# A scheduler's rule for a port shared by two engines, and an order searched anew: two transformer blocks on one core

## The chip, the cores and the metric

The kernel runs on one core of one Trainium2 chip. The metric is device time in microseconds (us), the median of three runs of the kernel before. A profiled execution gives the trace. Five engines matter: TensorE (PE; its weight loads are listed as PEld), VectorE (DVE), ScalarE (ACT), GpSimd (POOL) and SyncE (SP), which here only issues DMAs.

## The reference, cut to what matters

Batch 1, 256 tokens, width 1024, all float32. A first block with two layers (a sparse attention, then a block-wise attention) and a second block (feed-forward, two attentions side by side, feed-forward):

```python
cond = silu(c)
for i in range(2):                                   # first block
    shift, scale, gate = split(cond @ ada_w[i] + ada_b[i], 3)      # ada_w[i]: 1024 x 3072
    h = rms_norm(x, norm_g[i]) * (1 + scale) + shift               # "modulation"
    y = nsa_mixer(h, ...) if i == 0 else moba_mixer(h, ...)
    x = x + gate * y
# second block
x = x + 0.5 * swiglu(rms_norm(x, ffn1_norm), ...)    # 1024 -> 2816 -> 1024
h = rms_norm(x, mix_norm); proj = h @ w_in
x = x + (sigmoid(g_mla) * (mla(...) @ w_branch_mla) + sigmoid(g_fox) * (fox(...) @ w_branch_fox)) @ w_o
x = x + 0.5 * swiglu(rms_norm(x, ffn2_norm), ...)
```

In the attentions a softmax row p is divided by its sum (in the sparse attention also multiplied by a gate) before the product with the values.

## The kernel before

**Arithmetic.** A weight tile is loaded as float32 into `raw` (128x1024, six buffers), split into a high part `hi` (a rounded copy, ACT or DVE) and a low part `lo` = raw - hi (a subtraction, DVE or POOL). Activations lie transposed in `hT`, also as high and low part. A product is three matmuls (`mm3`): high by high, high by low, low by high. 512 columns of one take PE some 0.23 us at the higher clock.

**Stages.** The start: load x, norm statistics of each half of the tokens (`norm_stats`: ACT squares, DVE `nms`, POOL `rstd`), scale (`norm_x`), transpose on PE into `xT`. `mod0(q)` for q = 0..3 then makes a quarter of the first layer's modulation: `ada_mod(0, q)` (line 913) loads four tiles of `ada_w`, each 128x1024, `ada_sum` multiplies them with `sT` (silu of c) on PE, and `modulate` applies the result to two of the eight 128-wide pieces of `hT`. Each quarter is followed by three products with pieces of `nsa_w_in`. Later come the sparse attention (`nsa_scores`, `nsa_values`), its output product, the second layer (`moba_scores`, `moba_values`), feed-forward 1, the two attentions of the second block, feed-forward 2. Before each feed-forward `norm_T` makes h = x * rstd * gain (two DVE operations of 512 columns for each half of the tokens, tiles `t4` from `x` and `sh`), PE transposes it, ACT and DVE write `hT`. Nothing else is left to multiply there: PE has only the end of the product before as cover.

**What sets the order.** The code does not issue instructions itself; it calls a `Recorder`, which notes each operation, its predecessors and a cost. `order()` (line 380) then plays the program through on a model of the engines and takes, step by step, the instruction that can start first; among those ready at one time the one of lowest `rank`. `ORDER` (a permutation of some 1,150 units of work) sets the ranks, and `FLIPS` says for each operation that two engines could do (`either`, line 221) which one does it. Both tables were found by a search over the model's result. `emit` issues in that order, and each engine then runs its own list strictly in order. So everything depends on how the model sees waits: a wait that it does not see is not planned around.

**The port in the model.** `shared_port` (line 308) marks the operations of DVE and POOL that cannot run at the same time: every POOL operation with a tensor input in SBUF, and those of DVE with two such inputs, or plain copies and scalings from SBUF. A marked operation may start when `port[other]` is past. The lines in `order()` are

```python
if ops[i][6]:
    s = max(s, port[other[e]])
...
if c is None or (s, rank[i]) < c[:2]:
    c = (s, rank[i], i, e)
```

When POOL has waited for some time and DVE comes to the port just as it is given free, both have the same start `s`, and the lower rank goes.

**Clock and DMA in the model.** PE runs at 2.4 or 1.2 GHz; line 524 gives it the higher level where the work of the stretch before was at least 3060 (columns). `DMA_BPNS` is what all DMAs move in a nanosecond, 290 bytes.

**Row scalings.** `nsa_scores` (line 1310) and `moba_scores` (line 1485) scale each row block of `P` with its own `scale_rows`: 8 or 4 blocks of 128x128 where only one block of keys is seen (nk = 1, the first half of the tokens), else blocks of 128x256 or 128x128.

Of the kernel before, what the change touches and what calls it, by code (L numbers as in the profile page):

```python
# [11 lines left out]
AF = mybir.ActivationFunctionType  # L12
# [26 lines left out]
def shape_constants():  # L39
# [133 lines left out]
class Recorder:  # L173

    ENG = ("pe", "act", "dve", "pool", "sp")
    DMA_PRE = 1500.0
    DMA_LAT = 700.0
    DMA_BPNS = 290.0  # L180

    SETS = {AF.Exp: 1, AF.Tanh: 1, AF.Sin: 2, AF.Silu: 3}
    SET_LOAD = 1283.0

    def __init__(self, nc):
        self.nc = nc
# [1782 lines left out]
```

## Time and profile before

| | us |
|---|---|
| runs shown | 914.24, 917.89, 919.01 |
| median | 917.89 |
| profiled execution | 916.27 |
| its span (first to last instruction) | 914.4 |
| PE busy in the span | 871.4 |
| DVE, ACT, POOL busy | 662.3, 399.1, 406.0 |

PE is busy for 95% of the span; the mean granted clock is 0.981 of the higher level. "Busy" of DVE and POOL includes the time for which a started operation waits inside for the other of the two. Almost all instructions have the line of the recorder's `emit` (591, or 589 for a tiled group), so they are told apart by their tiles: `tp` is a PSUM bank for transposes and small products, `t` is `t4`, `w` is `w2`, `b` is `b4`, `f` is `f4`.

### The profile page before, as it was taken

To read this page: it belongs to the slowest core of one execution; us is meant where nothing else is said; L and a number is where in the kernel's file an instruction comes from. 1 tells how busy PE (TensorE), PEld (TensorE's weight loads), DVE (VectorE), ACT (ScalarE), POOL (GpSimd) and SP (SyncE) were. 2 spreads that over 40 slices of the span, in tenths; PEclk is the share of its full clock that TensorE was granted. 3 is DMA by queue.
4 is the path that set the end of the run, shared out by engine and by line. 5 is a ranking of instruction groups with operands and counts; after the bars stand their busy time and mean duration, and the time that the engine had idled before them with its cause. 6 is when DMAs were issued, how large, how long until landed. Compare 5 with 4: busy or idle time off the path is not lost.

```text
span 914.4 us, 13923 instructions
## 1 busy us (share of the span) xinstructions
PE 871.4 (95%) x4953; PEld 706.2 (77%) x4953; DVE 662.3 (72%) x1411; ACT 399.1 (44%) x858; POOL 406.0 (44%) x302
## 2 busy tenths in 40 slices
PE   5999999999999989999999999989999899999997
PEld 2579677767787758888888887877778888888886
DVE  5257889898788977766467676787897756666665
ACT  4245567875738742133412454464462323232221
POOL 3356442331354241155563736644535345451552
PEclk9899989999999998999999999999999999999999
DMA  8986656678444672656566556364435455656541
GB/s 256 320 273 185 229 163 179 186 229 265 157 139 128 220 233 90 194 184 202 167 186 199 163 164 176 119 179 144 140 116 190 132 182 179 214 176 195 160 162 47
DMA packets 129732, 165.08 MB, mean 181 GB/s; under 512 B 8055, under 2 KB 93433, under 8 KB 129662
## 3 DMA queue, kind: packets, MB, share of 16 engines
q1 hardware_dynamic: 129224, 164.07, 57.9%
q8 instruction: 39, 0.64, 0.3%
q14 instruction: 31, 0.25, 0.1%
q10 hardware_dynamic: 438, 0.12, 0.1%
HBM read 162.59 MB, written 1.05 MB: 179 GB/s over the span
## 4 chain that ended last, share of the span: by engine, by line
PE 78%; DVE 9%; ACT 4%; DMA 3%; issue 2%; POOL 2%; SPq 0%; POOLq 0%; ACTq 0%; DVEq 0%
PE mm L591 42%; PE tp L591 17%; PE s L591 9%; PE o L591 4%; PE o L589 3%; DVE lo L591 2%; PE s L589 2%; DVE t L591 2%; POOL lo L591 1%; ACT t L591 1%; DVE hi L591 1%; ACT w L591 1%; DVE w L591 1%; PE tp L589 1%; ACT hi L591 1%
## 5 line engine op out<-in xcount | busy, mean ns | idle before, releaser
L591 POOL TENSOR_TENSOR lo<-raw,hi 128x1024 fp32r<-128x1024 f32 (+2 forms) x94 | 232.9, 2483 | 236.2 <-DVE hi L591 121.9
L591 ACT ACTIVATE hi<-raw 128x1024 fp32r<-128x1024 f32 (+2 forms) x148 | 154.0, 1045 | 191.3 <-PE mm L591 77.8
L591 DVE TENSOR_TENSOR lo<-raw,hi 128x1024 fp32r<-128x1024 f32 (+3 forms) x155 | 196.8, 1275 | 29.5 <-ACT hi L591 28.6
L591 PE MATMUL mm<-hi,hT 128*128 128x512 f32 (+4 forms) x736 | 203.6, 354 | 2.6 <-DVE t L591 1.9
L591 PE MATMUL mm<-hT,hi 128*128 128x512 f32 (+1 forms) x576 | 170.1, 356 | 0.4 <-DVE w L591 0.4
L591 PEld LDWEIGHTS mm<-hi,hT 128*128 128x128 f32 x736 | 131.2, 193 | 24.2 <-issue 2.8
L591 PE MATMUL mm<-lo,hT 128*128 128x512 f32 (+4 forms) x368 | 129.4, 353 | 1.3 <-POOL lo L591 0.7
L591 PE MATMUL mm<-hT,lo 128*128 128x256 f32 x448 | 122.5, 288 | 1.0 <-DVE lo L591 1.0
L591 PE MATMUL tp<-hT,hi 128*128 128x512 f32 x320 | 115.8, 397 | 0.0
L591 PEld LDWEIGHTS mm<-hT,hi 128*128 128x128 f32 x576 | 102.5, 195 | 14.6 <-issue 1.6
L591 PE MATMUL mm<-hi,b 128*128 128x512 f32 (+2 forms) x272 | 96.2, 407 | 1.9 <-DVE b L591 1.8
L591 DVE CAST hi<-raw 128x1024 fp32r<-128x1024 f32 (+1 forms) x101 | 81.8, 816 | 21.0 <-PE s L591 6.8
L591 PEld LDWEIGHTS mm<-hT,lo 128*128 128x128 f32 x448 | 85.9, 193 | 6.6 <-DVE lo L591 2.5
L591 PE MATMUL tp<-hT,lo 128*128 128x256 f32 x320 | 83.7, 282 | 0.8 <-POOL lo L591 0.8
L591 PEld LDWEIGHTS mm<-lo,hT 128*128 128x128 f32 x368 | 71.1, 193 | 11.7 <-DVE lo L591 2.8
L591 PE MATMUL s<-hi,b 128*128 128x512 f32 x208 | 71.6, 395 | 0.0
L591 PEld LDWEIGHTS tp<-hT,hi 128*128 128x128 f32 x320 | 59.3, 188 | 11.6 <-ACT hi L591 0.2
L591 PEld LDWEIGHTS tp<-hT,lo 128*128 128x128 f32 x320 | 59.8, 188 | 5.6 <-POOL lo L591 1.3
L591 POOL TENSOR_TENSOR rstd<-hms,nhalf 128x4 f32<-128x4 f32 (+2 forms) x32 | 43.8, 1367 | 43.4 <-DVE hms L591 42.5
L591 PEld LDWEIGHTS mm<-hi,b 128*128 128x128 f32 (+1 forms) x272 | 51.6, 191 | 14.8 <-DVE b L591 2.4
L591 PE MATMUL mm<-lo,b 128*128 128x512 f32 (+1 forms) x136 | 55.3, 407 | 1.1 <-DVE lo L591 1.1
L591 ACT ACTIVATE t<-tt,nb 128x128 f32<-128x128 f32 (+1 forms) x96 | 42.5, 446 | 12.1 <-DVE nb L591 11.9
(281 smaller groups left out, 1389.5 us busy)
## 6 DMA issues: line engine op xcount, KB each, us to landing
raw<-in_ffn_w_gate SPq DMA_DIRECT2D x44, 512.0 KB, 4.6
raw<-in_ffn_w_up SPq DMA_DIRECT2D x44, 512.0 KB, 4.3
raw<-in_ffn_w_down SPq DMA_DIRECT2D x44, 512.0 KB, 4.1
raw<-in_ada_w SPq DMA_DIRECT2D x64, 256.0 KB, 4.6
raw<-in_nsa_w_in SPq DMA_DIRECT2D x26, 512.0 KB, 6.7
raw<-in_moba_w_in SPq DMA_DIRECT2D x20, 512.0 KB, 4.1
raw<-in_w_in SPq DMA_DIRECT2D x18, 512.0 KB, 4.1
raw<-in_ada_w SPq DMA_DIRECT2D x16, 512.0 KB, 4.3
```

The source lines that it names most:

```text
L589: self.engines[eng].matmul(**{n: real(v) for n, v in c.items()})
L591: getattr(self.engines[eng], fn)(*[real(v) for v in a], **{n: real(v) for n, v in k.items()})
```

## The change

Six things change; what is computed does not.

1. In `order()` an instruction that waits for the port keeps the time at which it asked (`asks`), and among engines whose next instructions have equal starts the one that asked first goes, before the rank.
2. The model's constants: the clock's condition goes from 3060 to 1200, `DMA_BPNS` from 290 to 320.
3. The `ada_w` tiles of the first layer go to `f4` (six buffers of the same size, which hold attention tensors later) and not to `raw`.
4. `modulate`'s DVE operation can also be given to ACT.
5. Where nk = 1, the 8 (sparse) or 4 (block-wise) scalings of 128x128 become one product of 128x1024 or 128x512 with the broadcast sums. There are four of each.
6. `ORDER` and `FLIPS` are searched anew on this model.

```diff
 ORDER = [
-    123, 454, 132, 942, 11, 5, 30, 249, 13, 99, 467, 4, 14, 950, 681, 307, 254, 0, 137, 46, 3, 10, 42, 274, 263, 21,
...
+    148, 10, 7, 304, 34, 695, 926, 234, 172, 452, 280, 446, 934, 660, 46, 238, 455, 649, 147, 652, 22, 666, 258, 0,
...
-    DMA_BPNS = 290.0
+    DMA_BPNS = 320.0
+    BUSY = 1200.0
...
-                        if ops[i][6]:
-                            s = max(s, port[other[e]])
                         for nm in of_bank[i]:
                             for e2, t in bank.get(nm, {}).items():
                                 if e2 != e:
                                     s = max(s, t + LAT[e2][e])
-                        if c is None or (s, rank[i]) < c[:2]:
-                            c = (s, rank[i], i, e)
+
+                        asks = s
+                        if ops[i][6]:
+                            s = max(s, port[other[e]])
+                        if c is None or (s, rank[i]) < (c[0], c[2]):
+                            c = (s, asks, rank[i], i, e)
...
-                    f = 2.4 if ticks.get(w - 1, 0.0) >= 3060.0 else 1.2
+                    f = 2.4 if ticks.get(w - 1, 0.0) >= self.BUSY else 1.2
...
         S.activation(hT[:, c, 0, ts], src, AF.Identity, scale=g, bias=sh)
-        V.tensor_scalar(u, src, g, sh, op0=OP.mult, op1=OP.add)
+        rec.either(("dve", "tensor_scalar", (u, src, g, sh), dict(op0=OP.mult, op1=OP.add)),
+                   ("act", "activation", (u, src, AF.Identity), dict(scale=g, bias=sh)))
...
-        ada_mod(0, q)
+        ada_mod(0, q, "f4")
...
-        for r in range(4):
+        if nk == 1:
+
+            V.tensor_tensor(P, P, sums.unsqueeze(3).unsqueeze(4).to_broadcast([128, 4, nb_, 1, 128]), op=OP.mult)
+        for r in range(4 if nk > 1 else 0):
...
-        for r in range(4):
+        if nk == 1:
+            V.tensor_tensor(P, P, sums.unsqueeze(2).unsqueeze(3).to_broadcast([128, 4, 1, 128]), op=OP.mult)
+        for r in range(4 if nk > 1 else 0):
             scale_rows(P[:, r], sums[:, r:r + 1], "act")
```

**The start, PE's list.** x0 and x1 are the two halves of the tokens. Before, PE's list after the first row broadcast (`w2_0` by `ones`) holds the sixteen transposes of x (`cst` by `w2`), then six groups of `ada_w` tiles:

```order
L591 MATMUL tp_1_120<-cst_0_123,w2_1_86 128x128 x4
L591 MATMUL tp_0_119<-cst_0_123,w2_2_87 128x128 x4
L591 MATMUL tp_1_120<-cst_0_123,w2_3_88 128x128 x4
L591 MATMUL tp_0_119<-cst_0_123,w2_4_89 128x128 x4
L589 MATMUL tp_1_120<-raw_5_68,sT_0_137 32x512 x2
L589 MATMUL tp_1_120<-raw_2_65,sT_0_137 32x512 x2
L589 MATMUL tp_1_120<-raw_0_63,sT_0_137 32x512 x2
L589 MATMUL tp_1_120<-raw_1_64,sT_0_137 32x512 x2
L591 MATMUL tp_0_119<-w2_5_90,ones_0_132 128x408
L591 MATMUL tp_1_120<-cst_0_123,w2_6_91 128x1 x4
L589 MATMUL tp_0_119<-raw_4_67,sT_0_137 32x512 x2
```

After, four groups of `ada_w` (from `f4`) stand ahead of the transposes, and twelve transposes and two more groups ahead of the first product:

```order
L589 MATMUL tp_1_120<-f4_0_104,sT_0_137 32x512 x2
L589 MATMUL tp_1_120<-f4_1_105,sT_0_137 32x512 x2
L589 MATMUL tp_1_120<-f4_2_106,sT_0_137 32x512 x2
L589 MATMUL tp_1_120<-f4_3_107,sT_0_137 32x512 x2
L591 MATMUL tp_0_119<-cst_0_123,w2_2_87 128x1 x4
L591 MATMUL tp_1_120<-cst_0_123,w2_1_86 128x128 x4
L591 MATMUL tp_0_119<-cst_0_123,w2_3_88 128x128 x4
L591 MATMUL tp_1_120<-cst_0_123,w2_4_89 128x128 x4
L589 MATMUL tp_0_119<-f4_4_108,sT_0_137 32x512 x2
L589 MATMUL tp_0_119<-f4_5_109,sT_0_137 32x512 x2
L591 MATMUL mm_0_114<-hi_0_69,hT_0_150 128x512
```

The four groups of the first quarter are now ahead of the wait for x; of the transposes four have moved behind the first products.

**The start, SP's list.** Before, one pair of `ada_w` pieces stands ahead of x:

```order
L591 DMA raw_0_63<-in_ada_w 128x2x256 x2
L591 DMA cols_0_122<-in_cols 128x56
L591 DMA x0_0_124<-in_x 128x1024
L591 DMA x1_0_125<-in_x 128x1024
L591 DMA raw_1_64<-in_nsa_w_in 128x2x512
L591 DMA raw_2_65<-in_ada_w 128x2x256 x2
L591 DMA raw_3_66<-in_nsa_w_in 128x2x512
```

After, the mask and four pairs do:

```order
L591 DMA mask_0_131<-in_cst2 128x256
L591 DMA f4_0_104<-in_ada_w 128x2x256 x2
L591 DMA f4_1_105<-in_ada_w 128x2x256 x2
L591 DMA cols_0_122<-in_cols 128x56
L591 DMA f4_2_106<-in_ada_w 128x2x256 x2
L591 DMA f4_3_107<-in_ada_w 128x2x256 x2
L591 DMA x0_0_124<-in_x 128x1024
L591 DMA x1_0_125<-in_x 128x1024
L591 DMA raw_0_63<-in_nsa_w_in 128x2x512
L591 DMA f4_4_108<-in_ada_w 128x2x256 x2
L591 DMA f4_5_109<-in_ada_w 128x2x256 x2
L591 DMA raw_1_64<-in_nsa_w_in 128x2x512
```

So x has moved behind 2.2 MB, and all six `f4` buffers are asked for before the second `raw`.

**Before feed-forward 1, DVE and POOL.** `t4` is the normed x that PE waits for, `mm` and `s0` are accumulators of the product before, `lo` belongs to weights that are needed later. Before, DVE:

```order
L591 TENSOR_TENSOR w2_5_90<-mm_2_116,gate_0_129 128x512
L591 TENSOR_TENSOR w2_1_86<-mm_1_115,gate_0_129 128x512
L591 TENSOR_TENSOR x1_0_125<-x1_0_125,w2_1_86 128x512
L591 TENSOR_TENSOR w2_0_85<-s0_0_117,gate_0_129 128x512
L591 TENSOR_SCALAR nms_1_144<-nss_2_142 128x1
L591 TENSOR_TENSOR lo_3_77<-raw_0_63,hi_3_72 128x1024
L591 SCALAR_TENSOR_TENSOR t4_2_98<-x0_0_124,rstd_3_149,sh_0_102 128x512 x2
```

The two `t4` of x0 stand in a row behind a `lo`. POOL in the same place, before:

```order
L591 TENSOR_TENSOR lo_2_76<-raw_5_68,hi_2_71 128x1024
L591 TENSOR_TENSOR x0_0_124<-x0_0_124,w2_5_90 128x512
L591 TENSOR_TENSOR rstd_3_149<-nms_1_144,nhalf_0_133 128x1
L591 TENSOR_TENSOR x1_0_125<-x1_0_125,w2_0_85 128x512
L591 TENSOR_TENSOR lo_0_74<-raw_1_64,hi_0_69 128x1024
L591 TENSOR_TENSOR rstd_0_146<-nms_2_145,nhalf_0_133 128x1
```

The two `rstd` (x0's, then x1's) stand around an addition to x1 and a `lo`. After, DVE:

```order
L591 TENSOR_TENSOR w2_2_87<-mm_1_115,gate_0_129 128x512
L591 TENSOR_TENSOR x0_0_124<-x0_0_124,w2_2_87 128x512
L591 TENSOR_TENSOR lo_2_76<-raw_3_66,hi_2_71 128x1024
L591 TENSOR_SCALAR nms_1_144<-nss_2_142 128x1
L591 TENSOR_TENSOR lo_0_74<-raw_1_64,hi_0_69 128x1024
L591 SCALAR_TENSOR_TENSOR t4_0_96<-x0_0_124,rstd_3_149,sh_0_102 128x512
L591 TENSOR_TENSOR w2_1_86<-mm_2_116,gate_0_129 128x512
L591 SCALAR_TENSOR_TENSOR t4_0_96<-x0_0_124,rstd_3_149,sh_0_102 128x512
```

x1's `w2_1` now stands between the two `t4`, and a `lo_0` of DVE ahead of them. After, POOL:

```order
L591 TENSOR_TENSOR x0_0_124<-x0_0_124,w2_6_91 128x512
L591 TENSOR_TENSOR x1_0_125<-x1_0_125,w2_0_85 128x512
L591 TENSOR_TENSOR rstd_3_149<-nms_1_144,nhalf_0_133 128x1
L591 TENSOR_TENSOR x1_0_125<-x1_0_125,w2_1_86 128x512
L591 TENSOR_TENSOR lo_3_77<-raw_0_63,hi_3_72 128x1024
L591 TENSOR_TENSOR rstd_0_146<-nms_2_145,nhalf_0_133 128x1
```

POOL's `lo` between `x1` and the second `rstd` has stayed one operation, but it is now behind an addition to x1 that waits for DVE's `w2_1`, which stands between the two `t4` of DVE; and the accumulators are finished in another order. Before, x0's last one is `mm_2` (by `w2_5`), with 16 products of 512 columns behind it in PE's list (six on `mm_1`, ten on `s0`); now it is `mm_1` (by `w2_2`), with 24 behind it, all on `mm_2`.

**Before feed-forward 2, DVE and POOL.** Before, DVE:

```order
L591 CAST hi_2_71<-raw_3_66 128x1024
L591 TENSOR_TENSOR x0_0_124<-mm_1_115,x0_0_124 128x512
L591 TENSOR_SCALAR nms_2_145<-nss_0_140 128x1
L591 SCALAR_TENSOR_TENSOR t4_2_98<-x0_0_124,rstd_1_147,sh_0_102 128x512 x2
L591 TENSOR_TENSOR x1_0_125<-mm_0_114,x1_0_125 128x512
```

The two `t4` stand in a row behind `nms_2`. POOL in the same place, before:

```order
L591 TENSOR_TENSOR lo_1_75<-raw_2_65,hi_1_70 128x1024
L591 TENSOR_TENSOR lo_2_76<-raw_3_66,hi_2_71 128x1024
L591 TENSOR_TENSOR rstd_1_147<-nms_2_145,nhalf_0_133 128x1
L591 TENSOR_TENSOR lo_4_78<-raw_4_67,hi_4_73 128x1024
L591 TENSOR_TENSOR rstd_2_148<-nms_0_143,nhalf_0_133 128x1
```

Each `rstd` has a `lo` behind it. After, DVE:

```order
L591 CAST hi_1_70<-raw_5_68 128x1024
L591 TENSOR_SCALAR nms_2_145<-nss_0_140 128x1
L591 TENSOR_TENSOR lo_0_74<-raw_5_68,hi_1_70 128x1024
L591 SCALAR_TENSOR_TENSOR t4_0_96<-x0_0_124,rstd_1_147,sh_0_102 128x512
L591 TENSOR_TENSOR x1_0_125<-s0_0_117,x1_0_125 128x512
L591 SCALAR_TENSOR_TENSOR t4_0_96<-x0_0_124,rstd_1_147,sh_0_102 128x512
L591 CAST hi_2_71<-raw_4_67 128x1024
```

A `lo_0` and an addition to x1 have come in ahead of and between the two `t4`, and a cast behind them. After, POOL:

```order
L591 TENSOR_TENSOR lo_3_77<-raw_4_67,hi_0_69 128x1024
L591 TENSOR_TENSOR rstd_1_147<-nms_2_145,nhalf_0_133 128x1
L591 TENSOR_TENSOR lo_2_76<-raw_4_67,hi_2_71 128x1024
L591 TENSOR_TENSOR rstd_2_148<-nms_0_143,nhalf_0_133 128x1
L591 TENSOR_TENSOR lo_2_76<-raw_5_68,hi_2_71 128x1024
```

Before, POOL's `lo_4` between the two `rstd` has its `hi` from ACT. After, the `lo_2` in its place needs `hi_2`, which DVE casts behind both `t4`. PE's list has 18 products of 512 columns behind x0's last accumulator before, 23 now.

## Rows read from the trace of the kernel before

**Rows 1.** The page's first part: busy time of each engine, share, instructions.

```profile
PE 871.4 (95%) x4953; PEld 706.2 (77%) x4953; DVE 662.3 (72%) x1411; ACT 399.1 (44%) x858; POOL 406.0 (44%) x302
```

**Rows 2.** Cores: span in us, mean granted clock as a share of 2.4 GHz.

```profile
core 0: 914.4 us, clock 0.981
```

**Rows 3.** Stretches: length, busy of PE, PEld, DVE, ACT, POOL, clock, DMA share, GB/s.

```profile
3.00:10.00 7.00, 2.04 (x2) 0.49 (x2) 3.19 (x17) 2.90 (x7) 0.89 (x2) 1.00 1.01 313
...
0.00:27.30 27.30, 14.93 (x53) 5.82 (x53) 13.79 (x45) 10.43 (x21) 9.35 (x16) 0.92 0.83 266
27.30:86.00 58.70, 58.69 (x327) 45.52 (x324) 29.48 (x69) 24.68 (x39) 30.53 (x28) 0.98 0.84 260
86.00:230.00 144.00, 135.80 (x974) 107.16 (x974) 128.42 (x385) 99.68 (x269) 51.61 (x70) 0.95 0.68 209
340.30:350.60 10.30, 6.36 (x29) 5.97 (x30) 8.75 (x10) 1.21 (x3) 5.93 (x4) 0.50 0.35 104
712.00:722.60 10.60, 8.22 (x40) 6.89 (x40) 8.11 (x10) 5.50 (x9) 5.14 (x4) 0.84 0.37 107
```

**Rows 4.** Timeline of PE, first 30 us: start, us, instruction, [idle before <- releaser].

```profile
11.76 3.44 PE L591 MATMUL tp<-cst,w 128*128 128x128 f32 x12 [4.41 <-ACT w L591]
...
24.02 3.35 PE L589 MATMUL tp<-raw,sT 128*32 128x512 f32 x8 [2.11 <-DMA raw<-in_ada_w]
27.30 0.80 PE L591 MATMUL s<-hi,hT 128*128 128x512 f32 x1
```

**Rows 5.** Timeline of ACT: the squares of the second half of x.

```profile
9.76 0.63 ACT L591 ACTIVATE t<-x 128x512 f32<-128x512 f32 x1 [1.65 <-DMA x<-in_x]
```

**Rows 6.** Timeline before feed-forward 1: DVE, POOL and PE.

```profile
334.16 2.42 POOL L591 TENSOR_TENSOR lo<-raw,hi 128x1024 fp32r<-128x1024 f32 x1
...
334.91 0.69 DVE L591 TENSOR_TENSOR w<-mm,gate 128x512 f32<-128x512 f32 x1 [1.85 <-ACT gate L591]
...
336.53 1.31 POOL L591 TENSOR_TENSOR x<-x,w 128x512 f32<-128x512 f32 x1
...
340.74 1.26 POOL L591 TENSOR_TENSOR x<-x,w 128x512 f32<-128x512 f32 x1
340.80 4.50 DVE L591 SCALAR_TENSOR_TENSOR t<-x,rstd,sh 128x512 f32<-128x512 f32 x2 [0.45 <-POOL rstd L591]
341.96 2.79 POOL L591 TENSOR_TENSOR lo<-raw,hi 128x1024 fp32r<-128x1024 f32 x1
...
342.60 1.12 PE L591 MATMUL tp<-cst,t 128*128 128x128 f32 x4 [4.23 <-DVE t L591]
...
345.35 0.90 PE L591 MATMUL tp<-cst,t 128*128 128x128 f32 x3 [1.64 <-DVE t L591]
```

**Rows 7.** The same before feed-forward 2.

```profile
713.47 3.52 DVE L591 SCALAR_TENSOR_TENSOR t<-x,rstd,sh 128x512 f32<-128x512 f32 x2 [0.67 <-POOL rstd L591]
...
717.05 1.09 PE L591 MATMUL tp<-cst,t 128*128 128x128 f32 x8 [1.90 <-DVE t L591]
```

**Rows 8.** Timeline: an operation of DVE beside POOL's `lo`, and PE behind it.

```profile
263.06 2.39 POOL L591 TENSOR_TENSOR lo<-raw,hi 128x1024 fp32r<-128x1024 f32 x1
...
263.16 2.44 DVE L591 TENSOR_TENSOR ropea<-w,rt 128x128 f32<-128x128 f32 x1
...
266.46 0.66 PE L591 MATMUL tp<-cst,w 128*128 128x128 f32 x4 [1.38 <-DVE w L591]
```

**Rows 9.** Timeline of PE: the first and the last of three later gaps.

```profile
611.79 0.39 PE L591 MATMUL mm<-hi,hT 128*128 128x264 f32 x1 [1.50 <-DVE t L591]
...
901.48 0.73 PE L591 MATMUL mm<-hi,b 128*128 128x512 f32 x2 [1.82 <-DVE b L591]
```

**Rows 10.** Groups by shape: count, busy us, mean ns of one, idle before.

```profile
L591 ACT ACTIVATE t<-t,sums 128x128 f32<-128x128 f32 x32 | 10.3, 394 | 2.6 <-DVE sums L591 2.6
...
L591 DVE TENSOR_SCALAR t<-t,sums 128x128 f32<-128x128 f32 x16 | 4.9, 349 | 0.0
...
L591 DVE TENSOR_TENSOR lo<-raw,hi 128x1024 fp32r<-128x1024 f32 x146 | 188.5, 1296 | 28.6 <-ACT hi L591 27.7
```

More of the change, by code (lines that the diff above doesn't have):

```diff
@@ L490, in order @@
                 raise RuntimeError("no instruction can go")
-            s, _, i, e = best
+            s, _, _, i, e = best
             dirty.clear()
```

149 rows, old and new, of tables (FLIPS, ORDER) are left out of this document.

## The prediction

> **What bounds the kernel now.** I read the part on busy time first: PE works for 871.4 of 914.4 us [rows 1], so at most 43.0 us of idle PE and the time that a low clock costs can be won by moving instructions. The mean granted clock is 0.981 [rows 2]; against the full level that is 0.019 x 914.4 = 17.4 us, since some 35 us of the span run at 1.2 GHz, where each product takes twice as long. PE's list keeps every product, so the question is only which of these 60 us go, and what comes instead.
>
> Next the stretches [rows 3], to see where PE idles. The first 27.30 us have 14.93 of PE, that is 12.4 idle; from there to 86 us PE is never idle. The two norms ahead of the feed-forwards stand out: 10.30 us with 6.36 of PE at clock 0.50, and 10.60 with 8.22 at 0.84. Then the timelines, to see what PE waits for in each.
>
> Before feed-forward 1 [rows 6] PE waits 4.23 and then 1.64 us for DVE's two `t`. Two of them took 4.50 us; one of 512 columns with two operands takes 0.69 (the product with the gate above it), so some 1.4 alone. Beside them POOL added to x (1.26) and made a `lo` (2.79): that is the port, given to POOL twice. The idle time is 5.87; and as PE has been idle, the next 10.3 us are granted 1.2 GHz [rows 3], so 6.36 us of work take 3.2 too long. This place costs 9.05.
>
> Before feed-forward 2 [rows 7] it is the same on a smaller scale: two `t` took 3.52, PE waits 1.90 and then in bits, 10.60 - 8.22 = 2.4 in all; the clock of 0.84 over 10.6 us is another 1.7 [rows 3]. This place costs 4.1.
>
> Four more gaps have the same form. At 263 us DVE's `ropea`, a 128x128 operation, took 2.44 beside POOL's `lo` of 2.39, and PE then waited 1.38 [rows 8]; three later waits, at 611, 622 and 901 us, are 1.50, 1.65 and 1.82 (first and last in [rows 9]). Sum 6.35. The rest of the idle time, 43.0 - 12.4 - 5.9 - 2.4 - 6.35 = 16, is the end and many small gaps.
>
> **The start.** Before, the second half of x is there at 9.76 [rows 5], the transposes run from 11.76, and then PE waits 2.11 us for `ada_w` until 24.02. The last such group needs 3.35 us at the low clock, and the first product starts at 27.30 [rows 4]. So the modulation's weights come last; x has long been there. The change turns this round: the mask and four pairs of `ada_w` (2.2 MB) land before x, where there was one pair (0.5 MB). In the first full stretch the DMAs move 313 GB/s [rows 3]: 1.7 MB more take 5.4 us, so the second half of x is there at 15.2. From it to the first product I take 6 us: norm and first transposes 2.0 (9.76 to 11.76), twelve transposes 3.44 [rows 4], the modulation of two pieces about 0.7. That is 21.2. The two groups of `ada_w` that still stand ahead of the product come behind another 1.6 MB (one product tile, two pairs), 5.1 us after x, at about 20.3 if the DMAs keep this rate, and take 1.1 to 3.35: 21.4 to 23.7. I take the first product at 22.3, a gain of 5.0. Bounds: 8 (19.3, if both chains run side by side at the full clock) and 0. For the latter speaks that all later loads have to come 5 us earlier as well: to 86 us the core moved 0.266 x 27.3 + 0.260 x 58.7 = 22.5 MB at a share of 0.84 [rows 3]; in 81 us that is 278 GB/s, a share of 0.9. It can be done, but with little left. That `ada_w` no longer occupies `raw` helps here, and I count it in this term alone.
>
> **Feed-forward 1.** Behind x0's last accumulator PE's list has 24 products instead of 16, 5.4 us instead of 3.6. Ahead of the `t` of x0, DVE and POOL have fewer operations at the port: POOL's `lo` cannot start between the two, because the addition to x1 ahead of it waits for `w2_1`, which DVE makes between them. The first `t` then no longer waits 1.1 for POOL's addition. So of 4.23 there remain 4.23 - 1.8 - 1.1 = 1.3, less some 0.6 of the 0.9 for which x0's own addition waited behind a `lo` (its `w` was there at 334.91 + 0.69, it began at 336.53): 0.7. The second `t` stands behind a product of the last accumulator and comes two operations of 0.69 after PE's end: about 1.3 of idle behind the first transposes. That leaves 2.0 of 5.87, and of the 3.2 lost to the clock I keep half, 1.7. Gain 9.05 - 3.7 = 5.3; bounds 8 (all but one) and 1 (the clock falls as before, and `lo` holds x1's `rstd` instead).
>
> **Feed-forward 2.** 23 products instead of 18 (5.2 instead of 4.1), and the `lo` between the two `rstd` needs a `hi` that DVE casts only behind both `t`: POOL cannot take the port there. Against it, an addition and a `lo` of DVE now stand ahead of or between the `t` (0.69, and 1.30 [rows 10]). Gain 3.0 of 4.1; bounds 4.1 and 0.
>
> **The other gaps.** The order is new everywhere, and the model now sees that POOL gets a port for which it asked first. If that is what made these four gaps, they shrink; but a new order throws the dice anew for all the small ones. I take 3.5 of 6.35; bounds a gain of 12 (these and a third of the 16) and a loss of 7 (as many again).
>
> **Scalings and modulation.** 48 scalings go: 32 on ACT at 394 ns, 16 on DVE at 349 ns [rows 10], 15.2 us. Eight products come, four of 1024 columns (three on DVE, one on POOL) and four of 512 (two and two). The nearest rows are the `lo`, two operands of 1024 columns: 1296 ns on DVE [rows 10], 2.39 on POOL [rows 8]. DVE: 3 x 1.30 + 2 x 0.69 = 5.3, about what it loses (4.9); POOL 5; ACT loses 10.3. Whether anything of it lies on the path the trace can't tell; DVE and POOL are busy for 72% and 44% [rows 1], ACT waits here and there for `sums`. I count 0, with bounds of a gain of 5 (ACT's eight in a row, 3.2 us, become one operation of 1.3: 1.9 saved at up to three of the places) and a loss of 19 (each of eight waits for one `lo`, 8 x 2.39). The six modulation operations that go to ACT lie beside a PE that is never idle up to 86 us: 0; without that cover each would cost some 0.4. The constants only steer the search.
>
> A rule of the Trainium skill speaks against the products. The page "SBUF — State Buffer", section "Who interferes with whom", says that the port which DVE and GpSimd share is an exclusive lock, that whoever issues first keeps it for the whole instruction ("Issue order, not op shape, decides who blocks"), and that PE and ACT never wait on anyone. The `ropea` of 2.44 us beside a `lo` of 2.39 [rows 8] agrees with it. By that rule the change moves 32 operations from an engine that never waits to the two that do; the rival on the products below has its price from rows.
>
> **Sum**, from the profiled execution, which took 916.27 us and so agrees with the median of 917.89 within 0.2%: -5.0 - 5.3 - 3.0 - 3.5 + 0 = -16.8, so 899.5; on the scale of the median 901.
>
> **Rivals.** (1) Only the start holds, the rest comes back elsewhere: shorter gaps before the feed-forwards, others where two blocks meet in a new order. 917.9 - 8 to 11: 907 to 910. For it: 16 us of small gaps show that no order is free of them. (2) The gains are larger: both norms are covered in full (8 and 4), the start gives 8, the four gaps go: about 890. For it: the model that the search used now sees this very wait. (3) The change doesn't do what it says: the lock in the model still differs from the chip, new stalls equal the old, and the start is bound by the DMAs: 916 to 918. For it: DMAs at 0.83 to 0.84 already [rows 3]. (4) The products are blocked: each waits for a `lo`, as `ropea` did, and PE waits with it, 8 x 2.39 = 19: 920. Against it: PE waited only 1.38 for that one [rows 8]. (5) Slower: the model now takes the high clock for granted at less work, so an order with more holes looks good to it, and the chip grants 1.2 GHz in more of the stretch up to 230 us, where it is 0.95 already [rows 3]. If the mean falls from 0.981 to 0.952, this costs 0.029 x 914 = 26.5: 927. It decides from a mean of about 0.957. Against it: after 230 us PE is nearly always full, and there is nothing to lower the clock.
>
> **How the numbers follow.** Forecast (893 to 907) 0.45; rival 1 0.23; rival 2 0.12; rival 3 0.10; rival 4 0.05; rival 5 0.05. The predicted time is the forecast's, 901. The range leaves out rivals 3 to 5, together 0.20, and reaches from 888 to 914. A measurement of this kernel can tell about 0.5% from no change, that is 913.3 and 922.5: faster 0.80 (forecast, rivals 1 and 2), same 0.15 (3 and 4), slower 0.05 (5).
>
> **What would show it.** In the changed kernel's profile: the first product at about 22 us, and PE full from there to 80; before the feed-forwards, two `t` of DVE at 0.7 us each, PE idle for at most 2 and 1 us, and a stretch at 1.2 GHz of at most 5 us; a mean clock of at least 0.985; PE idle for some 30 us. Wrong it would be if the first product came at 26 or later, if the `t` still took 2 us or more, if one of the products showed the length of a `lo` on DVE and PE waited behind it, or if the clock's mean fell.

## The result and the profile after

The changed kernel takes 884.0 us (881.2 to 886.3) against 917.5 us on the same chip: ratio 0.964 [0.960, 0.968], a gain of 33.5 us where 17 were forecast. The time lies below the range.

The page of after, first part (busy time, share, instructions), answers to [rows 1], and the cores (span, mean granted clock) to [rows 2]:

```profile
PE 856.9 (97%) x4953; PEld 697.8 (79%) x4953; DVE 641.8 (73%) x1366; ACT 421.6 (48%) x882; POOL 393.3 (44%) x283
```

```profile
core 0: 884.5 us, clock 0.994
```

The span is 29.9 us shorter. PE's products are the same 4953, yet its busy time fell by 14.5 us (871.4 to 856.9); idle PE fell by 15.4 (43.0 to 27.6). So about half of the gain is not a wait that went but products that ran shorter: the clock lost 17.4 us before, and after loses 0.006 x 884.5 = 5.3. The traces' records of the clock begin only at 19.5 us in before and at 11.9 in after, and the column shows 1.00 ahead of them. Before's twelve transposes at 11.76 took 3.44 us [rows 4], where eight take 1.05 at 2.4 GHz (below, 700.03), so the 17.4 are somewhat too few.

To see where, both spans are cut at the same places of the program: the first product, the first transposes of the two feed-forwards' norms, the end. The columns are those of [rows 3]: length, busy time (and instructions) of PE, PEld, DVE, ACT, POOL, granted clock, DMA share, GB/s. Before (its first stretch stands in [rows 3]):

```profile
27.30:342.60 315.30, 300.13 (x1923) 235.60 (x1920) 252.84 (x679) 193.15 (x468) 130.61 (x138) 0.97 0.66 206
342.60:717.05 374.45, 365.85 (x1963) 302.41 (x1963) 267.63 (x517) 144.70 (x289) 182.13 (x107) 0.99 0.53 164
717.05:914.40 197.35, 190.45 (x1020) 162.38 (x1020) 128.04 (x172) 50.84 (x80) 83.88 (x42) 0.99 0.51 160
```

After:

```profile
0.00:24.04 24.04, 12.35 (x46) 5.55 (x46) 12.39 (x43) 10.18 (x20) 5.55 (x13) 0.82 0.93 317
24.04:322.89 298.85, 291.93 (x1930) 231.34 (x1926) 246.92 (x661) 196.21 (x468) 123.38 (x122) 1.00 0.67 211
322.89:690.62 367.73, 364.09 (x1962) 300.25 (x1963) 260.21 (x506) 153.10 (x301) 171.43 (x104) 1.00 0.56 169
690.62:884.50 193.88, 188.54 (x1021) 160.65 (x1019) 122.30 (x159) 62.11 (x96) 92.97 (x44) 1.00 0.53 165
```

The start gives 3.3 us, the second stretch 16.4, the third 6.7, the last 3.5. In the second, idle PE falls from 15.2 to 6.9 and busy PE by 8.2, at a clock that rises from 0.97 to 1.00: half of the whole gain, in a stretch of which the sum of the prediction had only FFN1's share and a part of the one gap of [rows 8].

The stretch of 0.95 from 86 to 230 us of [rows 3] held three pieces at 1.2 GHz (same columns, before):

```profile
118.46:125.29 6.83, 6.12 (x27) 5.75 (x28) 5.97 (x23) 3.84 (x14) 1.11 (x2) 0.50 0.69 209
179.90:183.30 3.40, 3.40 (x19) 3.40 (x18) 2.34 (x7) 3.40 (x10) 0.62 (x1) 0.50 0.70 197
193.56:196.97 3.41, 3.41 (x9) 2.65 (x8) 3.16 (x17) 3.06 (x16) 2.72 (x2) 0.50 0.89 276
```

What came ahead of the first of them is the form of [rows 8] (timeline of before: start, us, instruction, idle before and its releaser):

```profile
114.68 3.64 POOL L591 TENSOR_TENSOR lo<-raw,hi 128x1024 fp32r<-128x1024 f32 x1 [0.66 <-ACT hi L591]
...
116.28 2.44 DVE L591 TENSOR_SCALAR t<-t,sums 128x256 f32<-128x256 f32 x2
...
118.51 0.74 PE L591 MATMUL tp<-cst,t 128*128 128x128 f32 x2 [0.38 <-DVE t L591]
```

DVE's two scalings needed 2.44 us beside POOL's `lo` (one of this shape took 0.34 just ahead of them, at 115.75). PE waited only 0.38 for them, with waits of 0.41 and 0.47 shortly before (at 115.13 and 115.88), and 6.8 us from 118.46 on ran at half speed. After shows 1.2 GHz only around its start, from 15.3 to 25.5 us.

The place that answers to [rows 6], before feed-forward 1 (timeline of after):

```profile
320.75 0.56 POOL L591 TENSOR_TENSOR rstd<-nms,nhalf 128x1 f32<-128x1 f32 x1 [2.46 <-DVE nms L591]
...
322.09 0.75 DVE L591 SCALAR_TENSOR_TENSOR t<-x,rstd,sh 128x512 f32<-128x512 f32 x1
322.75 0.68 DVE L591 TENSOR_TENSOR w<-mm,gate 128x512 f32<-128x512 f32 x1
...
322.89 0.66 PE L591 MATMUL tp<-cst,t 128*128 128x128 f32 x4 [0.66 <-DVE t L591]
323.35 0.74 DVE L591 SCALAR_TENSOR_TENSOR t<-x,rstd,sh 128x512 f32<-128x512 f32 x1
323.51 1.72 POOL L591 TENSOR_TENSOR x<-x,w 128x512 f32<-128x512 f32 x1 [2.20 <-DVE w L591]
...
324.15 0.33 PE L591 MATMUL tp<-cst,t 128*128 128x128 f32 x1 [0.60 <-DVE t L591]
```

Each `t` takes 0.75 (4.50 for two before); POOL waits until `w` is there, so its addition (323.51) asks behind the second `t` (323.35). PE waits 0.66 and 0.60 instead of 4.23 and 1.64. Before feed-forward 2 ([rows 7]) the two `t` now take 0.75 each, and PE waits 0.32 behind the first transpose:

```profile
691.21 0.99 PE L591 MATMUL tp<-cst,t 128*128 128x128 f32 x7 [0.32 <-DVE t L591]
```

### The profile page after: what moved, and what is told of

Same layout as the page of the kernel before. It is cut to its first block, busy times and chain, and to the rows that moved or that the text cites. A ratio compares the mean times of both kernels' runs of the same rounds, so it can differ in the third digit from the quotient of the medians.

```text
span 884.5 us, 13884 instructions
## 1 busy us (share of the span) xinstructions
PE 856.9 (97%) x4953; PEld 697.8 (79%) x4953; DVE 641.8 (73%) x1366; ACT 421.6 (48%) x882; POOL 393.3 (44%) x283
## 3 DMA queue, kind: packets, MB, share of 16 engines
HBM read 162.59 MB, written 1.05 MB: 185 GB/s over the span
## 5 line engine op out<-in xcount | busy, mean ns | idle before, releaser
L591 POOL TENSOR_TENSOR lo<-raw,hi 128x1024 fp32r<-128x1024 f32 (+1 forms) x87 | 217.0, 2498 | 210.7 <-ACT hi L591 103.8
L591 DVE TENSOR_TENSOR lo<-raw,hi 128x1024 fp32r<-128x1024 f32 (+4 forms) x162 | 214.1, 1328 | 43.2 <-ACT hi L591 41.8
L591 ACT ACTIVATE hi<-raw 128x1024 fp32r<-128x1024 f32 (+3 forms) x163 | 169.8, 1047 | 145.0 <-PE mm L591 64.4
L591 PE MATMUL mm<-hT,hi 128*128 128x512 f32 (+1 forms) x576 | 166.9, 351 | 0.0
L591 PEld LDWEIGHTS mm<-hi,hT 128*128 128x128 f32 x736 | 128.6, 189 | 28.6 <-ACT hT L591 5.7
L591 PE MATMUL mm<-lo,hT 128*128 128x512 f32 (+4 forms) x368 | 126.3, 346 | 0.0
L591 PEld LDWEIGHTS mm<-hT,hi 128*128 128x128 f32 x576 | 100.0, 189 | 13.7 <-issue 0.6
L591 PE MATMUL mm<-hi,b 128*128 128x512 f32 (+2 forms) x272 | 93.7, 400 | 1.4 <-ACT hi L591 0.9
L591 DVE CAST hi<-raw 128x1024 fp32r<-128x1024 f32 (+3 forms) x86 | 75.8, 887 | 13.8 <-PE mm L591 4.5
L591 PE MATMUL mm<-lo,b 128*128 128x512 f32 (+2 forms) x136 | 54.1, 398 | 0.1
```

The costliest lines, as they stand in the source:

```text
L591: getattr(self.engines[eng], fn)(*[real(v) for v in a], **{n: real(v) for n, v in k.items()})
```

## The experiments

Three theories stood after the result. **Lock:** the gain comes from the order in which DVE and POOL get the port, everywhere; the model now plans the order that the chip takes. **Products:** 48 scalings less, and operations moved to other engines, shorten the way. **Buffers and start:** `ada_w` in `f4` and earlier lets all later work begin earlier.

### Before's order with the port's order made right

Played through in the model of before, the plan lets POOL's addition to x1 ahead of FFN1, which asks for the port at 328.05, go behind DVE's second `t`, which asks at 329.18. The chip gave the port to POOL, who asked first [rows 6]. There are 31 such places in before's plan and none in after's. Here POOL gets a tiny operation ahead of each of the 31, which reads one column of what DVE makes there, so that POOL asks behind DVE, as planned. `ORDER` and `FLIPS` are those of before.

```diff
         for i in self.order():
+            if i in HOLDS:          # {POOL's operation: DVE's that the plan put first}, 31 pairs
+                hold(i)             # tensor_tensor(note[:p, n:n + 1], first, first, op=OP.add)
```

> The kernel before with its order, flips and buffers unchanged. In the plan of the kernel before there are 31 places where a POOL operation was ready for the shared port before an operation of DVE, and yet was planned behind it. In each of them POOL first adds one column of that DVE operation's result to itself (a scratch tile, some 0.2 us), so that it cannot take the port ahead of DVE. Theory 'lock' (the surplus over the forecast is the port given to POOL against the plan, and the 1.2 GHz stretches that follow these gaps): the two t of DVE before feed-forward 1 take 1.4 us instead of 4.50, PE waits there at most 3 instead of 5.9; the same before feed-forward 2, 1.4 instead of 3.52 and less than 0.7 of idle; the 1.2 GHz stretch at 118 to 125 us goes; in all 14 to 22 us off, 896 to 904 us. Rival 'order' (the gain lies in products that now cover the norms and in the changed parts, not in who gets the port): the t get short, but PE waits as before; at most 5 off, 912 or more.

Measured: 896.9, ratio 0.980 [0.977, 0.982], 18.8 us faster than before, though POOL has 31 operations more. Before feed-forward 1 and 2:

```profile
331.89 1.41 DVE L608 SCALAR_TENSOR_TENSOR t<-x,rstd,sh 128x512 f32<-128x512 f32 x2 [0.45 <-POOL rstd L608]
...
332.70 1.78 PE L608 MATMUL tp<-cst,t 128*128 128x128 f32 x8 [3.24 <-DVE t L608]
333.39 0.19 POOL L598 TENSOR_TENSOR hold<-t 128x1 f32<-128x1 f32 x1 [1.53 <-DVE t L608]
...
698.51 1.41 DVE L608 SCALAR_TENSOR_TENSOR t<-x,rstd,sh 128x512 f32<-128x512 f32 x2 [0.67 <-POOL rstd L608]
...
700.03 1.05 PE L608 MATMUL tp<-cst,t 128*128 128x128 f32 x8
```

Two `t` take 1.41 instead of 4.50 and 3.52. Before FFN2 PE waits for nothing; before FFN1 for 3.24, where after waits 1.26: the other 2 us are the new order's eight products more of cover. The stretches, cut as above:

```profile
25.23:332.70 307.47, 294.76 (x1922) 231.03 (x1920) 244.28 (x679) 192.52 (x468) 127.70 (x148) 0.99 0.68 211
332.70:700.03 367.33, 364.72 (x1963) 301.32 (x1963) 256.98 (x516) 144.62 (x289) 180.10 (x121) 1.00 0.55 167
700.03:894.10 194.07, 189.39 (x1021) 161.12 (x1020) 123.16 (x172) 50.84 (x80) 84.92 (x47) 1.00 0.54 164
```

From FFN1 to the end this is after (367.3 and 194.1 against 367.7 and 193.9): there the port's order is the whole gain. In the second stretch it gives 7.8 of 16.4. A rule of the Trainium skill fits this ("SBUF — State Buffer", "Who interferes with whom": of the shared port, "Issue order, not op shape, decides who blocks"). By that rule a scheduler that lets rank decide between two waiting engines plans what the chip won't do; the 18.8 us agree.

### One of the 31 alone

If a gap of 0.38 us at 118.5 costs 3.4 us of clock, one hold on the `lo` at 114.68 should bring it back.

```diff
+HOLDS = {1150: 834}     # POOL's lo at 114.68 waits for DVE's lo behind the scalings
```

> The kernel before with one such hold only: POOL's lo that DVE's scalings of t by sums meet at 114.7 to 118.3 us (two of them took 2.44 us there) waits until DVE's lo planned ahead of it is done. Theory 'lock': the scalings take 0.34 us each, the small waits of PE around them (0.38 and 0.66 us) and the stretch at 1.2 GHz from 118.46 to 125.29 us (6.12 us of busy PE, 3.1 lost) go: 3 to 4.5 us off, 913 to 914.5. Rival 'order': the stretch is slow because its operations are small; clock and time stay, 916.5 to 918.5.

Measured: 914.9 against 915.8, ratio 1.000 [0.998, 1.001]. The expectation failed.

```profile
116.55 2.41 POOL L608 TENSOR_TENSOR lo<-raw,hi 128x1024 fp32r<-128x1024 f32 x1
...
117.69 1.30 DVE L608 TENSOR_SCALAR cmx<-cmx 128x8 f32<-128x8 f32 x1
...
123.51 0.33 PE L608 MATMUL tp<-cst,pc 128*128 128x128 f32 x1 [1.61 <-POOL pc L608]
```

The two scalings took 0.60 together, and the stretch at 118 us is gone. But the `lo` now met DVE's next operation at the port (128x8, 1.30 us), POOL's `pc` came late behind it, PE waited 1.61, and a stretch of 3.4 us at 1.2 GHz began at 124.02 instead. The kernel with all 31 holds has the same collision and the same wait, and no such stretch behind it (timeline, then the stretch in the columns of above):

```profile
123.07 0.33 PE L608 MATMUL tp<-cst,pc 128*128 128x128 f32 x1 [1.61 <-POOL pc L608]
```

```profile
123.07:130.00 6.93, 6.93 (x62) 6.20 (x64) 5.77 (x10) 5.62 (x12) 3.52 (x3) 1.00 0.57 187
```

So the collision moved on in both, and whether the clock falls behind a given wait these runs don't explain. One place repaired alone brings nothing that can be measured here.

### The parts alone: the products

After's order, but each of the eight products is issued as the 8 or 4 row scalings that it replaced, two of three on ACT.

```diff
         for i in self.order():
+            if i in self.split:      # the eight products
+                for q, (p, f) in enumerate(self.split[i]):
+                    if q % 3 == 2: nv.tensor_scalar(p, p, f, None, op0=OP.mult)
+                    else: ns.activation(p, p, AF.Copy, scale=f)
+                continue
```

> The changed kernel in its own order, but each of the eight products of P with the row sums is issued, at its place, as the 8 or 4 row scalings of before (two of three on ACT, one of three on DVE). Theory 'lock', and the zero of the prediction: within 2 us of the changed kernel, 882 to 886. Rival 'products' (the surplus over the forecast comes from fewer operations in the attentions): 7 to 12 us slower than the changed kernel, 891 to 896.

Measured: 890.8, ratio 0.973 [0.971, 0.975]: some 6.6 us slower than after once more (below; by the ratios to before), between the two expectations, all of it in the stretch ahead of FFN1 (305.0 instead of 298.85 us). The reverse is before with the 31 holds and the products in it, each where the first of its scalings stood:

```diff
+            if i in at:                       # first of its row scalings
+                p, f = at[i]
+                self.engines["dve"].tensor_tensor(p, p, f, op=OP.mult)
+            if i in drop: continue
```

> The kernel before with the 31 holds of e1_holds, and besides each group of 8 or 4 row scalings replaced by one product on DVE at the place of its first scaling. Theory 'products': they are worth some 6 us by themselves, as undoing them in the changed kernel suggests (890.8 against 884.0); this gives 890 to 892. Rival 'fit': those 6 us were the price of putting eight operations where the new order had room for one; in the old order the products give 0 to 2 us, 895 to 897.

Measured: 904.3, ratio 0.989 [0.987, 0.991]: worse than either expectation, 7.4 us slower than the holds alone by the medians, 8.5 by the ratios. The groups and PE's timeline:

```profile
L609 DVE TENSOR_TENSOR t<-t,sums 128x512 f32<-128x512 f32 x4 | 4.8, 1200 | 0.0
...
125.49 0.47 PE L619 MATMUL tp<-cst,pc 128*128 128x128 f32 x1 [3.49 <-POOL pc L619]
...
197.61 0.45 PE L619 MATMUL tp<-cst,t 128*128 128x128 f32 x1 [2.40 <-DVE t L609]
```

The four of 512 columns take a mean of 1.20 us, since one of them took 2.36 at 273.76 (another 0.69), which looks like a wait at the port, and the two waits of PE are 1.61 and 1.03 in the kernel with the holds alone. Products in the order made for scalings lose 7 to 8 us, scalings in the order made for products lose 6.6. So the products have no gain of their own that these runs show. A third reading, that an order fits the durations for which it was searched, agrees with both; it is argued from them, and no run tests it by itself.

### The parts alone: buffers and modulation

Before's order, `ada_w` in `f4`; and after's order, with six of `modulate`'s operations put back from ACT to DVE.

```diff
+        for q, z in enumerate(sorted(first, key=first.get)):   # the 16 ada_w tiles
+            self.tiles[z][0] = "f4"
+            self.place[z] = q % 6
```

```diff
+        swap = {1805, 1842, 1845, 1851, 1863, 1869}     # modulate's six on ACT
         for i in self.order():
+            if i in swap: eng, fn, a, k = self.alts[i][:4]; ...   # issued on DVE
```

> The kernel before in its own order, but the 16 tiles of the first layer's ada_w lie in the six f4 buffers in turn and not in raw. Theory: at the start the order of the loads decides, not the buffers, since the DMAs are busy for 0.83 to 0.9 of the time: first product at 27 us as before, 916 to 919. Rival 'buffers': loads were held back by raw, the first product comes 3 to 5 us earlier, 912 to 915.

> The changed kernel with the six modulation operations that went to ACT back on DVE, at their places. They stand at 213 to 217 us of the second layer (not in the first 86 us, where the prediction put them), and PE waits 1.21 us there for ACT's hT. Theory of the prediction: 0, 883 to 885. Rival 'ACT is late there': with six operations of 0.4 us less on ACT the gap closes, 0.5 to 1.2 us faster. Rival 'DVE is late there': DVE has the additions of x and the low parts, 0.5 to 2 us slower.

Measured: 915.3, ratio 1.000 [0.998, 1.001], against before; 884.5, ratio 0.967 [0.965, 0.969], which is after's time. Neither can be told from zero. With the buffers alone the first product does come earlier, at 22.64 instead of 27.30, as the rival in the expectation had it:

```profile
22.64 0.80 PE L598 MATMUL s<-hi,hT 128*128 128x512 f32 x1 [0.16 <-ACT hT L598]
...
27.18 1.65 PE L596 MATMUL tp<-f,sT 128*32 128x512 f32 x8 [1.61 <-DMA f<-in_ada_w]
```

Six products later PE waits 1.61 us for the next `ada_w`, whose place in the list of loads hasn't changed; of the 4.7 us 2.3 are left at 86 us (the same product starts at 84.14 and 86.45), and none that can be measured at the end. So an earlier first product alone isn't yet time. The prediction placed the six modulation operations in the first 86 us; they belong to the second layer, at 217 to 229 us in after. PE's wait of 1.21 for an `hT` of ACT, at 216.80, lies ahead of them and is there with them on DVE, too.

### The start

In after POOL's `lo` reaches the port 0.09 us ahead of DVE's modulation, and DVE's operation of 128x2 then takes 2.27 us, with a scaling of x behind it. In another profile of the same kernel DVE was first, by 0.7 us. Timelines of after, and of after once more:

```profile
17.47 2.35 POOL L591 TENSOR_TENSOR lo<-raw,hi 128x1024 fp32r<-128x1024 f32 x1 [0.75 <-ACT hi L591]
17.56 2.27 DVE L591 SCALAR_TENSOR_TENSOR mods<-mods,cols 128x2 f32<-128x2 f32 x1
19.75 0.47 DVE L591 TENSOR_SCALAR w<-x,rstd 128x512 f32<-128x512 f32 x1
...
24.04 0.80 PE L591 MATMUL mm<-hi,hT 128*128 128x512 f32 x1
```

```profile
16.12 0.16 DVE L591 SCALAR_TENSOR_TENSOR mods<-mods,cols 128x2 f32<-128x2 f32 x1
16.20 0.49 DVE L591 TENSOR_SCALAR w<-x,rstd 128x512 f32<-128x512 f32 x1
16.85 2.36 POOL L591 TENSOR_TENSOR lo<-raw,hi 128x1024 fp32r<-128x1024 f32 x1 [0.76 <-ACT hi L591]
...
20.05 0.50 PE L591 MATMUL mm<-hi,hT 128*128 128x512 f32 x1
```

A hold of POOL's `lo` behind DVE's scaling makes the race certain; a second kernel also gives the other engine two operations ahead of the longest gaps left.

```diff
+HOLDS = {113: 34}        # both: POOL's lo waits for DVE's scaling of x
+        swap = {529, 1103}       # second kernel alone: issued on their other engine
```

> The changed kernel with one hold: POOL's first lo, which takes the port at 17.47 us and keeps DVE's mods (2.27 us) and the scaling of x behind it waiting, comes behind that scaling. Theory 'lock': the scaling ends at about 18.2 instead of 20.2, the transposes of x1 and the first product follow 1.5 us earlier (22.5 instead of 24.04), 882 to 883 in all. Rival: the lo itself (now at 18.4 to 20.8) or the ada_w of the next quarter (landed by 22) is what the first products wait for next; 884, no change.

> As e5_start, and two operations of 512 columns go from POOL (1.25 us) to DVE (0.69) at their places, for which PE waits 1.44 us at 88.41 and 1.04 us at 139.87. Theory: 0.6 us of each gap go, and 1 to 3 us in all against the changed kernel, 881 to 883. Rival: DVE, which runs its list in order, now waits for the DMA or the operand in their place, and the gaps stay: as e5_start.

> The changed kernel once more, as the mark for the runs on this chip. If the start is a race (POOL's first lo and DVE's mods come to the port within 0.1 us of each other at 17.4 us, and in two other kernels with the same start DVE came first), its first product comes at 24.0 in some profiles and at 21.5 in others; 881 to 885 in all.

Measured: 884.0, ratio 0.967 [0.965, 0.969]; 883.6, ratio 0.966 [0.964, 0.968]; after once more 884.4, ratio 0.966 [0.963, 0.969]. No gain from either. With the hold the first product came at 21.71, inside what after shows anyway (20.05 to 24.04); in the second kernel the two gaps shrank from 1.44 and 1.04 us to 0.84 and 0.87. Of the 4.0 us between the two profiles of after, the wait at the port is 2.1. The first half of x came 0.6 later (first squares at 13.23 and 12.60), and the remaining 1.3 lie on the way through PE, whose clock was 0.60 from 13 us to the first product in the one and 0.76 in the other.

### What a stretch at 1.2 GHz costs

Before's order, PE's wait ahead of the norms filled with repeated products (13 ahead of FFN1, 7 ahead of FFN2) into a bank that the transposes overwrite: the waits for DVE stay, PE is busy.

```diff
+            if i in fill:            # {first transpose: (a product before it, 13 or 7 times)}
+                for _ in range(times):
+                    pe.matmul(b, lhsT=real(k["lhsT"]), rhs=real(k["rhs"]), start=True, stop=True)
```

> The kernel before in its own order, with idle products in PE's list: 13 of 512 columns (0.227 us each) ahead of the first transposes before feed-forward 1, 7 ahead of those before feed-forward 2, into the bank that the transposes then overwrite. The waits for DVE's t stay; PE is busy in them. Theory 'the clock falls because PE was idle': no stretch at 1.2 GHz from 340 to 350 us and none from 719, 2.5 to 5 us faster, 910 to 913. Rival 'the clock falls there for another reason, or the products themselves delay the transposes': 914.5 or more.

Measured: 915.6 (12 runs), ratio 0.999 [0.997, 1.001]: 1.3 us, interval -0.5 to 3.0, for a mean clock that rose from 0.984 to 0.989, some 4 us by the conversion that the prediction used. The time is the rival's, while the clock did most of what the theory said: the 1.2 GHz stretch before FFN2 went, and that before FFN1 became shorter (3.4 us from 346.2, for 10.2):

```profile
338.78 3.11 PE L603 MATMUL tp<-hi,b 128*128 128x512 f32 x13
...
343.19 0.66 PE L609 MATMUL tp<-cst,t 128*128 128x128 f32 x4 [1.30 <-DVE t L609]
...
345.95 0.94 PE L609 MATMUL tp<-cst,t 128*128 128x128 f32 x4 [2.10 <-DVE t L609]
```

PE still waits for `t`, and in this place a faster PE only waits longer. Part of what a low clock takes from PE is thus hidden by a wait that is there anyway. How much of the gain of 33.5 us is clock in the sense that it would have come without the waits' going, the runs don't settle.

The same at the start of after. A first try, with the hold of the start, placed the repeated `ada_w` products behind the reload of their buffers:

```diff
+                for _ in range(2): ...   # the four tiled ada_w products, behind the DMAs that refill f4
```

> The changed kernel with the hold of e5_start and with the last four ada_w products of the first quarter repeated twice (2.1 us) into the next bank, in the 2.9 us for which PE waits from 12.6 to 15.5 us. Theory: no 1.2 GHz at the start in any run, 0 to 4 us off a run, 1 to 2 in the median: 880 to 883. Rival: the clock at the start costs nothing, since DVE, ACT and the loads set the first product there; as after_again.

```profile
28.36 2.57 PE L615 MATMUL tp<-f,sT 128*32 128x512 f32 x5 [15.47 <-DMA f<-in_ada_w]
```

PE waited 15.47 us for a load; the first product came at 37.67, 17.6 us later than in the second profile of after, and the time was 897.8, 13.4 us longer. It says nothing on the clock, but shows that a later start costs: 0.76 us for each us by the medians, 0.90 by the two profiles' spans (895.7 against 879.8). The second try has 2 x 4 repeated products ahead of the reload, and the hold of the start:

```diff
+            if i == 161:
+                for _ in range(2): ...   # the four tiled products of the group before, again
```

> As e11_start_fill, but the repeated ada_w products stand right behind the originals in the order of issue, ahead of the reload of their buffers (in e11_start_fill they came behind it, so that PE waited until 28.4 us for the next quarter's weights and the first product came at 37.7). Theory: PE is busy from 8 to 14.8 us, nothing at 1.2 GHz at the start, first product at 20 to 21.5 us in each profile, 1 to 2 us off the changed kernel's 884.4 (ratio to before 0.964 to 0.965). Rival: at the start the loads and the chain of x set the time, the clock costs nothing there; as the changed kernel, 0.966.

Measured: 881.8 (880.7 to 883.6), ratio 0.962 [0.960, 0.964]; the clock is 0.997 to 1.000 in all its runs. It is faster than after with the hold alone (0.967 [0.965, 0.969]), and by some 0.4% than after once more, where the intervals just touch. The first product is at 19.73, and from the first record of the clock, at 12.89, on the start is at 2.4 GHz:

```profile
0.00:19.73 19.73, 12.57 (x63) 4.84 (x63) 9.67 (x40) 9.38 (x19) 5.71 (x14) 1.00 0.90 302
```

The hold alone has the same race made certain and x at the same time (first squares at 13.04 and 13.00), and its first product comes 2.0 us later. Its column also shows 1.00 for the start, but the trace has no record of the clock there ahead of 21.50. PE's eight tiled products ahead of the first product tell the two apart, first with the hold alone, then with the repeated products:

```profile
19.98 1.79 PE L606 MATMUL tp<-f,sT 128*32 128x512 f32 x8
21.71 0.50 PE L608 MATMUL mm<-hi,hT 128*128 128x512 f32 x1
```

```profile
18.59 1.21 PE L612 MATMUL tp<-f,sT 128*32 128x512 f32 x8
19.73 0.50 PE L614 MATMUL mm<-hi,hT 128*128 128x512 f32 x1
```

So the 2.0 us are PE's speed, in one profile of each, and the medians are 884.0 and 881.8. This is the fastest of the kernels, by little over after, whose own interval reaches to it.

## Why the prediction was off

The terms, from the two profiles:

| term | predicted | measured |
|---|---|---|
| start (first product) | -5.0 (0 to -8) | -3.3 (-7.3 in the second profile of after) |
| before feed-forward 1 | -5.3 (-1 to -8) | -7.8 (idle 5.87 to 1.26; clock 3.2 to 0) |
| before feed-forward 2 | -3.0 (0 to -4.1) | -3.2 (idle 2.4 to 0.9; clock 1.7 to 0) |
| the other gaps | -3.5 (+7 to -12) | -15.6, the rest of 29.9 |
| scalings, modulation | 0 (+19 to -5) | none by themselves |
| sum | -16.8 | -29.9 |

**The mechanism was right.** What the prediction wanted to see is there: two `t` of 0.75 us, PE idle for 1.3 and 0.9 us before the feed-forwards, nothing at 1.2 GHz there, a mean clock of 0.994, PE idle for 27.6 us. The 31 holds show that the port's order does more than half of it (18.8 us of 33.5).

**The step that failed is the size of the other gaps.** Two things were left out of that term. First, it took as places of the lock only the four waits that are over 1.3 us, and for the rest "a new order throws the dice anew". But before's plan has 31 places, spread over the whole program, and the rule empties them all at once. Of PE's gaps of 0.4 us and more outside the start and the two norms, 15.6 us before, 6.9 remain, and the four of [rows 8] and [rows 9] are gone. With the 31 holds alone they are gone as well, and 8.1 us of such gaps remain. Second, the clock of 0.95 from 86 to 230 us stood in [rows 3] and was used only as a danger (rival 5), never as a gain: 0.05 x 144 = 7.2 us, and the three stretches shown above lost (6.83 + 3.40 + 3.41) / 2 = 6.8. With the holds alone one of the three is left, 3.4 us long (from 186.5). Idle 15.6 - 6.9 = 8.7 and clock 6.8 make the 15.6 of the table within 0.1. Even the bound of 12 was drawn from idle time alone.

**The start** came short of its term in this profile and beyond it in the other: the second half of x was squared at 14.50 (15.2 predicted), and then a race of 0.1 us at the port (2.1 us) and the clock of PE made 24.04 of what could be 20.05. The bounds were right, and the cause of the spread was not foreseen. How much of an earlier first product reaches the end isn't known either: with the buffers alone 4.7 us of it brought nothing.

**Feed-forward 1** was taken as half cured of the low clock; it is cured in full. In the stretch from FFN1 to FFN2 PE's busy time fell by only 1.8 us, though, with 3.2 counted for the clock there. That agrees with the filled gaps, and means that single clock terms are good to a factor of two here; the sum over the span (PE busy 14.5 less) is not in doubt.

**The rivals.** The second (all gains larger, 890) came nearest, and still lacks the clock of the rest. The fourth (products blocked) did not come: three on DVE took 1.22 us each, and POOL's two of 512 columns 1.04. The holds give 7.8 of the 16.4 us that the stretch ahead of FFN1 gained. What of the other 8.6 is the new order and what the new rule can't be told: the old tables don't make an order under the new rule, so neither was tried alone. The two constants were not tried alone either.

## What to carry to other kernels

Where two engines share a port, compare at each place who asks first with who is planned first. Here 31 such differences cost 18.8 us together, in the waits and in the clock behind some of them, while one of them repaired alone brought nothing that could be measured. Put the clock of every stretch into the sum, as a gain too, not only that of the gaps that catch the eye. An order searched for one set of durations is worth less with another: changing eight operations in it, in either direction, lost some 7 us.

## What the runs showed of the hardware that was not expected

A tiny operation pays the whole wait at the port: 128x2 took 2.27 us and 128x8 1.30 us on DVE behind POOL's `lo` of 2.4, where 128x2 takes 0.16 alone. A wait of 1.61 us ahead of the same product was followed by 3.4 us at 1.2 GHz with one hold and by none with 31, and a wait of 1.44 us at 88.41 us of after by none. So the length of a gap alone doesn't tell whether the clock falls. And the DMAs moved more than the 313 GB/s from which the start was estimated: 371 GB/s from 13 to 24 us of after.
